# Three column tiles of the second ConvGLU as plain products, with part of the Winograd operands made later

## Chip, cores and metric

The kernel runs on one core of a Trainium2 chip. The metric is the device time of one execution in microseconds (us), median of several. The core has a matrix engine (PE, with its weight loads PEld), VectorE (DVE), ScalarE (ACT), GpSimd (POOL) and SyncE (SP), which here only issues DMAs. Each engine works off its own queue in order; a semaphore wait at the head of a queue holds everything behind it.

## What is computed

Two layers over 512 latent tokens and 256 context tokens of width 1024: layer 0 is windowed attention and a ConvGLU, layer 1 a bidirectional gated recurrence (HGRN) and a ConvGLU. The change is in the ConvGLU of layer 1, on the latent tokens alone:

```
hx2 = rms_norm(x, norm2_g) * (1 + sc2) + sh2          # x: 512 x 1024
gate, val = split(hx2 @ w_up)                         # w_up: 1024 x 5632
u = silu(dwconv3(gate, conv_w, conv_b)) * val         # 512 x 2816
x = x + g2 * (u @ w_down)                             # w_down: 2816 x 1024
```

## The kernel before, in words

Everything lies transposed: features on partitions, tokens along the free dimension. Each fp32 operand is split in two parts, high (`wh`, or index 0 of `hs`) and low (`wl`, index 1), and each product is three matmuls: high by high, high by low, low by high. The high part is a copy on ScalarE, the low part a subtraction on DVE.

The up product has 22 column tiles (`ft`), each with 128 gate columns and 128 value columns. Each is one step of a Strassen-Winograd scheme: the 1024 input features are halved (k below 4, k from 4 on), the tokens are halved (258 columns each, the last of which hold the shift column and padding), and gate and value are the halves of the output. So `gate_pair` (L917) makes 7 products of 4 k-tiles and 3 terms, 84 matmuls of 258 columns, where plain products need 96. The sums on the weights are made by `load_pair` (L121): 7 operands with a high and a low part each (L140, L141) and 4 sums (L136), in a temporary `s1` and in the raw weight buffer `wr` itself. The sums on the activations are made once by `halves` (L361) and `combos` (L386): four quarters of the scaled input (b11, b12 for the first features, b21, b22 for the second; the second index is the token half), and of these seven operands `hs[0..6]`: 0, 1 and 4 are the quarters b11, b21 and b22; 2, 3, 5 and 6 are combinations.

The row factor R (the inverse norm of each token) is only multiplied in after the product, so products can start before the norm is known. `row_factor` (L529) sums the squares on PE (`nss`), takes the power on GpSimd, and spreads the result over the partitions (`dg`, then PE's `nR`, then a copy).

Before this stage, `hgrn_out` (L1297) computes the HGRN output in 4 pairs of row tiles (dp and dp + 4): 8 k-tiles each in PSUM (`ho`), then the residual add into `xl` (L914), then `halves` and the first part of `combos` for the pair, then the squares for the norm. The rest of `combos` (operands 5 and 6) comes after the loop. The `y` buffers of `halves` lie in the pool `ot`, which is closed after the stage; its memory goes on to pools of the ConvGLU.

`ffn` (L964) works in rounds of column tiles, for layer 1 by `ROUNDS[1]` (4, 4, 4, 4, 4, 2). In each round the up tiles of the next round (`up`) alternate with four pairs of down products (`dn`) of the tiles at hand. After a tile's products `up` does the gate's convolution, SiLU and product on ScalarE and DVE and splits the result into `g`. Each up tile loads 1 MB of weights on SyncE's queue into one of two raw buffers (`wr`); the down weights go to `wd` on the same queue. Prepared weight operands rotate through the pools `ws0`, `wsC`, `wsD`, `wsE`. PSUM has 8 banks in two pools of four; `bank` takes them in turn.

The order of the instructions on each queue is not written by hand: a scheduler with its own timing model takes the ready instruction that stands first in the program; weight preparation is moved 180 places forward (`W_AHEAD`). What it fixes is then the order in which the engines run.

Of the kernel before, what the change touches and what calls it, by code (L numbers as in the profile page):

```python
# [9 lines left out]
F32R = mybir.dt.float32r  # L10
BF16 = mybir.dt.bfloat16
AF = mybir.ActivationFunctionType
# [15 lines left out]
NFF = DFF // P  # L28
EPS = 1e-6
NEG = -1e30  # L30
ROUNDS = ((3, 3, 4, 4, 3, 5), (4, 4, 4, 4, 4, 2))
W_AHEAD = 180
PER_UNIT = 3.2

# [34 lines left out]
def f(t):  # L69
    return t.bitcast(F32)  # L70


class Kernel:
# [307 lines left out]
    def put(self, op, kk, src):  # L381

        self.nc.scalar.activation(op[:, 0, kk], src, AF.Copy)  # L383
        self.nc.vector.tensor_tensor(op[:, 1, kk], src, f(op[:, 0, kk]), op=ALU.subtract)

    def combos(self, ys, kk, hs):  # L386


        nc = self.nc
        (b11, b12), (b21, b22) = ys  # L390

        def put(i, src):
            self.put(hs[i], kk, src)

        def diff(o, x, y):
            nc.vector.tensor_tensor(o, x, y, op=ALU.subtract)
            return o

        put(0, b11)
        put(1, b21)  # L400
        put(4, b22)
        t1 = diff(b12, b12, b11)
        put(2, t1)
        t2 = diff(b22, b22, t1)
        put(3, t2)
        yield
        put(5, diff(b21, b21, t2))
        put(6, diff(b11, t2, b11))

    def late_combos(self, l, w, kk, half, hs, pool):  # L410

# [502 lines left out]
            self.nc.vector.scalar_tensor_tensor(x[:, d], ps[:, lo:hi], self.modc(l, v, which, d), x[:, d], op0=ALU.mult, op1=ALU.add)  # L914


    def gate_pair(self, ft, ops, hs, G, gg, R, rows, half, tmp, bank):  # L917


        nc = self.nc  # L920
        Z, Y, V = (bank(x)[:, 0:half] for x in ("pZ", "pY", "pV"))

        def prod(i, ps, first=False):
            self.product(ps, ops[i], lambda k: (hs[i][:, 0, k], hs[i][:, 1, k]), 4, first)

        g = (G[:, 1:1 + half], G[:, 1 + half:1 + 2 * half], gg[:, 0:half], gg[:, half:])
        t0, t2 = (tmp.tile([P, half], F32, tag="t", name="t", bufs=2) for _ in range(2))
        add = lambda o, x, y: nc.vector.tensor_tensor(o, x, y, op=ALU.add)  # L928
        times = lambda eng, o, x, y: eng.tensor_tensor(o, x, y, op=ALU.mult)  # L929

        prod(0, Z, True)
        nc.scalar.activation(t0, Z, AF.Copy)  # L932
        prod(1, Y, True)
        add(g[0], t0, Y)
        prod(3, Z)
        nc.scalar.activation(g[2], Z, AF.Copy)
        next(rows, None)
        if ft == 0:
            prod(2, Z)
            nc.scalar.activation(t2, Z, AF.Copy)  # L940
            prod(4, Z)
            prod(6, V, True)
            nc.scalar.activation(g[3], V, AF.Copy)
            prod(5, V)
        else:
            prod(6, V, True)
            nc.scalar.activation(g[3], V, AF.Copy)
            prod(2, Z)
            nc.scalar.activation(t2, Z, AF.Copy)
            prod(5, V)  # L950
            prod(4, Z)
        add(g[3], g[3], t2)
        add(g[2], g[2], V)
        for _ in rows:
            pass

        times(nc.vector, g[0], g[0], R[:, 0:half])
        times(nc.vector, g[1], Z, R[:, half:])
        times(nc.gpsimd, gg, gg, R)

    def ffn(self, l, hs, R, rows, lat_only, tmp, acp, bk, gp, done, side=None):
# [14 lines left out]
        def up(ft):  # L976

            ws_ = [self.wcols(wup, ft * P, P), self.wcols(wup, DFF + ft * P, P)]
            ops = self.load_pair(ws_, tmp)
            if side:  # L980
                next(side, None)

            G = tmp.tile([P, 2 * half + 2], F32, tag="G", name="G", bufs=gb)
            gg = tmp.tile([P, 2 * half], F32, tag="ny", name="gg", bufs=2)
            self.gate_pair(ft, ops, hs, G, gg, R, rows, half, tmp, bank)
            nc.scalar.activation(ap(G[:, 0:1], 0, (TW + 1, nv)), G[:, 1 + SH:1 + SH + nv], AF.Copy)
            cb = tmp.tile([P, 2], F32, tag="cb", name="cb")
            nc.scalar.activation(cb[:, :nv], G[:, 1 + SH:1 + SH + nv], AF.Identity, scale=ws[:, ft:ft + 1], bias=cw[:, 66 + ft:67 + ft])
            u = tmp.tile([P, n], F32, tag="nt", name="u", bufs=gb)
            nc.scalar.activation(u, G[:, 1:1 + n], AF.Copy, scale=cw[:, 22 + ft:23 + ft])  # L990
            nc.vector.scalar_tensor_tensor(u, G[:, 0:n], cw[:, ft:ft + 1], u, op0=ALU.mult, op1=ALU.add)
            nc.vector.scalar_tensor_tensor(u, G[:, 2:2 + n], cw[:, 44 + ft:45 + ft], u, op0=ALU.mult, op1=ALU.add)
            for v, c, m in segs:
                nc.scalar.activation(u[:, c:c + m], u[:, c:c + m], AF.Silu, bias=cb[:, v:v + 1])
                nc.vector.scalar_tensor_tensor(gg[:, c:c + m], gg[:, c:c + m], gg[:, SH + v:SH + v + 1], u[:, c:c + m],
                                               op0=ALU.subtract, op1=ALU.mult)
            g2 = gp.tile([P, 2, n], F32R, tag="g", name="g")
            nc.scalar.activation(g2[:, 0], gg[:, :n], AF.Copy)  # L998
            nc.vector.tensor_tensor(g2[:, 1], gg[:, :n], f(g2[:, 0]), op=ALU.subtract)
            return g2  # L1000

        f0, late = 0, None
        gt = [up(ft) for ft in range(ROUNDS[l][0])]
        for r, nf in enumerate(ROUNDS[l]):


# [289 lines left out]

    def hgrn_out(self, part, hs, acc, tmp, pj):  # L1297
        nc = self.nc
        some = []
        wout = self.a["hgrn_w_out"][0]  # L1300
        oh = part[0]
        act = lambda k: (oh[:, 0, k], oh[:, 1, k])
        for dp in range(KT // 2):
            if dp < 2:
                w, ps, ks = part[1][dp], part[2][dp], (KT - 1,)
            else:
                w = self.load_w([self.wcols(wout, d * P, P) for d in (dp, dp + 4)])
                ps = pj.tile([P, 1024], F32, tag="pj", name="ho")
                ks = range(KT)
            for j in range(2):  # L1310
                d = dp + 4 * j
                pd = ps[:, 512 * j:512 * j + 512]
                for _ in self.mm_steps(w[j], ks, act, [(pd, 0)], first=dp >= 2):
                    pass
                self.add_gated(1, 2, d, pd, True)
            some.append(self.combos(self.halves(1, 1, dp, 258, True, tmp, ("y0", "y1"), 4), dp, hs))
            next(some[-1])
            for d in (dp, dp + 4):
                self.square_acc(d, acc, True, tmp, "sg", first=(d == 0))
        for rest in some:  # L1320
            for _ in rest:
                pass


    def dump(self, name, t):
# [3 lines left out]
    def run(self, stop=99):  # L1329
# [75 lines left out]
        pj = self.pool(e2, "pj", 2, PSUM)  # L1405
        part = self.hgrn(hn2[0], R, accs[0], hb, pj, lv, sc)
        hc = self.pool(rs, "hC", 1, right=True)
        hs1 = hc.tile([P, 7, 2, 4, 258], F32R, tag="hs", name="hs3")
        hs = [hs1[:, i] for i in range(7)]
        ot = self.pool(es, "ot", 1)  # L1410
        acc = Rp.tile([P, LAT], F32, tag="acc", name="acc2")
        self.hgrn_out(part, hs, acc, ot, pj)
# [94 lines left out]
```

## Time and profile before

| what | us |
|---|---|
| median of 3 runs | 1810.76 |
| lowest and highest run | 1810.32, 1812.5 |
| the profiled execution | 1809.72 |
| its span, first to last instruction | 1807.9 |

In the profile, a row of the timeline gives the start in us from the span's start, the duration, the engine, the line of the kernel, the operation, output and input tile names, and how many instructions it merges; a bracket at its end is the idle time before it and what released it. PE's durations overlap, since matmuls are pipelined: their cost is the distance from start to start. In the stretches by window each engine has its busy time and, in brackets, its number of instructions. PEclk is the clock that was granted to PE as a share of 2.4 GHz.

### The profile page before, as it was taken

To read this page: it belongs to the slowest core of one execution; us is meant where nothing else is said; L and a number is where in the kernel's file an instruction comes from. 1 tells how busy PE (TensorE), PEld (TensorE's weight loads), DVE (VectorE), ACT (ScalarE), POOL (GpSimd) and SP (SyncE) were. 2 spreads that over 40 slices of the span, in tenths; PEclk is the share of its full clock that TensorE was granted. 3 is DMA by queue.
4 is the path that set the end of the run, shared out by engine and by line. 5 is a ranking of instruction groups with operands and counts; after the bars stand their busy time and mean duration, and the time that the engine had idled before them with its cause. 6 is when DMAs were issued, how large, how long until landed. Compare 5 with 4: busy or idle time off the path is not lost.

```text
span 1807.9 us, 32327 instructions
## 1 busy us (share of the span) xinstructions
PE 1760.6 (97%) x13062; PEld 1543.7 (85%) x13062; DVE 1324.9 (73%) x2420; ACT 840.5 (46%) x1754; POOL 248.7 (14%) x233
## 2 busy tenths in 40 slices
PE   6999999999999999999999999999998899999998
PEld 4968785788889989999998888888986689999997
DVE  6576767467768675868877766777776799999985
ACT  4354556555534443534455333333332555555553
POOL 1233333200100010100011110111110011111110
PEclk9999999998999999999999999999999999999999
DMA  9250005232343343312213212111126133433222
GB/s 309 79 200 35 24 1 187 59 105 71 120 126 106 108 131 104 100 47 82 62 52 103 69 48 59 45 51 50 46 71 210 47 106 105 117 106 105 86 68 81
DMA packets 204611, 166.44 MB, mean 92 GB/s; under 512 B 5341, under 2 KB 198446, under 8 KB 199342
## 3 DMA queue, kind: packets, MB, share of 16 engines
q1 hardware_dynamic: 196800, 160.47, 28.9%
q10 hardware_dynamic: 7662, 3.92, 0.8%
q8 instruction: 102, 1.67, 0.4%
q14 instruction: 47, 0.39, 0.1%
HBM read 162.27 MB, written 2.10 MB: 91 GB/s over the span
## 4 chain that ended last, share of the span: by engine, by line
PE 87%; DMA 5%; DVE 5%; ACT 2%; issue 1%; SPq 0%; ACTq 0%; DVEq 0%
PE dn L170 16%; PE pZ L188 15%; PE pf L170 8%; PE pV L188 7%; PE pjq L611 4%; PE pv L170 4%; PE ao L170 4%; PE pY L188 3%; PE pgate L170 3%; PE pq L170 3%; PE pv L844 2%; PE ho L170 2%; PE pt L836 2%; PE kv L611 2%; DMA wr<-in_ffn_w_up 2%; PE ada L309 2%
## 5 line engine op out<-in xcount | busy, mean ns | idle before, releaser
L188 PE MATMUL pZ<-hs,wh 128*128 128x386 f32 (+1 forms) x1408 | 314.1, 314 | 1.1 <-ACT t L932 0.9
L140 ACT ACTIVATE wh<-wr 128x512 fp32r<-128x512 f32 x264 | 162.3, 628 | 229.3 <-PE pZ L188 73.7
L170 PE MATMUL dn<-g,wh 128*128 128x512 f32 (+1 forms) x1056 | 266.9, 358 | 0.4 <-ACT g L998 0.3
L188 PEld LDWEIGHTS pZ<-hs,wh 128*128 128x128 f32 x1408 | 240.7, 191 | 11.5 <-issue 3.4
L117 ACT ACTIVATE wh<-wr 128x512 fp32r<-128x512 f32 (+2 forms) x192 | 113.3, 601 | 292.0 <-PE pf L170 84.0
L141 DVE TENSOR_TENSOR wl<-wr,wh 128x512 fp32r<-128x512 f32 x264 | 189.5, 728 | 47.2 <-ACT wh L140 46.3
L188 PE MATMUL pZ<-hs,wl 128*128 128x386 f32 (+1 forms) x704 | 218.2, 313 | 0.8 <-DVE wl L141 0.8
L170 PEld LDWEIGHTS dn<-g,wh 128*128 128x128 f32 x1056 | 173.4, 188 | 27.6 <-ACT g L998 0.9
L929 POOL TENSOR_TENSOR gg<-gg,R 128x772 f32<-128x772 f32 (+1 forms) x44 | 87.4, 1986 | 722.8 <-DVE gg L928 657.8
L118 DVE TENSOR_TENSOR wl<-wr,wh 128x512 fp32r<-128x512 f32 (+2 forms) x192 | 129.8, 684 | 71.0 <-ACT wh L117 53.5
L188 PE MATMUL pV<-hs,wh 128*128 128x386 f32 (+1 forms) x704 | 161.0, 314 | 1.8 <-ACT hs L383 1.8
L170 PE MATMUL dn<-g,wl 128*128 128x512 f32 (+1 forms) x528 | 160.0, 356 | 0.3 <-DVE wl L118 0.3
L188 PEld LDWEIGHTS pZ<-hs,wl 128*128 128x128 f32 x704 | 133.4, 190 | 3.8 <-DVE wl L141 1.9
L188 PEld LDWEIGHTS pV<-hs,wh 128*128 128x128 f32 x704 | 121.2, 191 | 5.8 <-ACT hs L383 2.1
L170 PE MATMUL pf<-hn,wh 128*128 128x512 f32 (+1 forms) x512 | 117.5, 344 | 0.5 <-ACT v L1114 0.5
L188 PE MATMUL pV<-hs,wl 128*128 128x386 f32 (+1 forms) x352 | 110.2, 314 | 1.3 <-DVE wl L141 1.2
L170 PEld LDWEIGHTS dn<-g,wl 128*128 128x128 f32 x528 | 88.0, 188 | 14.5 <-DVE wl L118 0.5
L1033 DVE SCALAR_TENSOR_TENSOR xl<-dn,mod,xl 128x512 f32<-128x512 f32 x96 | 71.1, 746 | 38.4 <-PE dn L170 38.1
L170 PEld LDWEIGHTS pf<-hn,wh 128*128 128x128 f32 x512 | 79.4, 189 | 12.4 <-ACT v L1114 0.6
L188 PE MATMUL pY<-hs,wh 128*128 128x386 f32 (+1 forms) x352 | 80.8, 315 | 3.9 <-ACT hs L383 3.4
L611 PE MATMUL pjq<-wh,hn 128*128 128x256 f32 x384 | 76.3, 290 | 0.3 <-DVE mod L324 0.3
L188 PEld LDWEIGHTS pV<-hs,wl 128*128 128x128 f32 x352 | 67.1, 191 | 4.5 <-DVE wl L141 1.8
(301 smaller groups left out, 3850.4 us busy)
## 6 DMA issues: line engine op xcount, KB each, us to landing
wr<-in_ffn_w_up SPq DMA_DIRECT2D x88, 512.0 KB, 5.2
wada<-in_ada_w SPq DMA_DIRECT2D x40, 1024.0 KB, 4.8
wr<-in_hgrn_w_in SPq DMA_DIRECT2D x40, 512.0 KB, 4.0
wd<-in_ffn_w_down SPq DMA_DIRECT2D x20, 512.0 KB, 4.0
ar<-in_ada_w SPq DMA_DIRECT2D x32, 256.0 KB, 7.0
wr<-in_attn_w_in SPq DMA_DIRECT2D x6, 1024.0 KB, 8.3
wr<-in_ffn_w_down SPq DMA_DIRECT2D x12, 384.0 KB, 3.0
wr<-in_attn_w_out SPq DMA_DIRECT2D x8, 512.0 KB, 4.0
```

Source lines behind the costliest of these rows:

```text
L117: nc.scalar.activation(wh, src, AF.Copy)
L118: nc.vector.tensor_tensor(wl, src, f(wh), op=ALU.subtract)
L140: nc.scalar.activation(ops[i][0], src, AF.Copy)
L141: nc.vector.tensor_tensor(ops[i][1], src, f(ops[i][0]), op=ALU.subtract)
L170: nc.tensor.matmul(o, lhsT=wt, rhs=at[:, t0:t0 + o.shape[1]], start=(first and n == 0 and i == 0), stop=(last and n == len(ks) - 1 and i = ...
L188: self.nc.tensor.matmul(ps, lhsT=wt, rhs=at, start=(first and k == 0 and i == 0), stop=(k == nk - 1 and i == 2), skip_group_check=not first)
L309: nc.tensor.matmul(ps[32 * j:32 * j + 32, 0:512], lhsT=self.cs[:, k, :], rhs=raw[:, j * 512:(j + 1) * 512], start=(k == 0), stop=(k == KT ...
L611: nc.tensor.matmul(out, lhsT=x, rhs=y[:, wk], start=(start and k == 0 and j == 0), stop=(stop and k == KT - 1 and j == 2))
L836: nc.tensor.transpose(pt[:, j * P:(j + 1) * P], pr[j][:, b * P:(b + 1) * P], self.ident)
L844: nc.tensor.matmul(pv[a * HD:(a + 1) * HD, 0:256], lhsT=V[:, tl, g, :], rhs=pT[:, a * 256:(a + 1) * 256], start=(b == 0), stop=(b == len(t ...
L929: times = lambda eng, o, x, y: eng.tensor_tensor(o, x, y, op=ALU.mult)
L1033: nc.vector.scalar_tensor_tensor(x[:, d], o, self.modc(l, v, 5, d), x[:, d], op0=ALU.mult, op1=ALU.add)
```

## The change

In layer 1 alone:

- The first three column tiles (`PLAIN = 3`) take plain products (`gate_plain`) with ordinary weight operands (`load_w`: 4 of 512 columns, high and low) instead of a Winograd step. For gate and value each, two PSUM tiles (one per token half) are accumulated side by side over 8 k-tiles, in the order 0, 4, 1, 5, 2, 6, 3, 7. R is multiplied in at the end of the value product, for gate and value, by four DVE operations that read PSUM.
- They read the quarters straight: `hs` has eight operands now, and b12 stands in `hs[7]`. The quarters are made in `hgrn_out` by `quadrants`, from `xl` into high and low part without the intermediate `y`; shift columns and padding of the second token half once by `quadrant_shifts`.
- `combos` makes only operands 2, 3, 5 and 6 there (`quadrants=False`), with `halves` into buffers of the `g` pool, issued in the program ahead of column tile 0 (pairs 0 and 1) and ahead of tile 1 (pairs 2 and 3).
- `ROUNDS[1]` is (3, 4, 4, 4, 4, 3).
- The scratch memory that the compiler reserves for DMAs is cut to 1024 bytes a partition.

```diff
-ROUNDS = ((3, 3, 4, 4, 3, 5), (4, 4, 4, 4, 4, 2))
+ROUNDS = ((3, 3, 4, 4, 3, 5), (3, 4, 4, 4, 4, 3))
+PLAIN = 3
...
-        put(0, b11)
-        put(1, b21)
-        put(4, b22)
+        if quadrants:
+            put(0, b11)
+            put(1, b21)
+            put(4, b22)
...
+    def quadrants(self, l, w, d, half, hs):
+        nc = self.nc
+        sc = self.gs[l][:, 0, 8 * w + d:8 * w + d + 1]
+        for op, t0, n in ((hs[1 if d >= 4 else 0], 0, half), (hs[4 if d >= 4 else 7], half, LAT - half)):
+            x, h = self.xl[:, d, t0:t0 + n], op[:, 0, d % 4, 0:n]
+            nc.scalar.activation(h, x, AF.Copy, scale=sc)
+            nc.vector.scalar_tensor_tensor(op[:, 1, d % 4, 0:n], x, sc, f(h), op0=ALU.mult, op1=ALU.subtract)
+
+    def quadrant_shifts(self, l, w, half, hs):
+        nc = self.nc
+        c = SH - half
+        for op, d in ((hs[7], 0), (hs[4], 4)):
+            sh = ap(self.mod[l][:, 0, 24 * w + d:24 * w + d + 1], 0, (1, 4), (48, 2))
+            y = op[:, 0, :, c:c + 2]
+            nc.scalar.activation(y, sh, AF.Copy)
+            nc.vector.tensor_tensor(op[:, 1, :, c:c + 2], sh, f(y), op=ALU.subtract)
+            nc.gpsimd.memset(f(op[:, :, :, c + 2:]), 0.0)
...
+    def gate_plain(self, ft, ops, hs, G, gg, R, rows, half, tmp, bank):
+        nc = self.nc
+        quad = ((hs[0], hs[1]), (hs[7], hs[4]))
+        for j, dst in enumerate((G[:, 1:1 + 2 * half], gg)):
+            ps = [bank("pd")[:, 0:half] for _ in range(2)]
+            for k in (0, 4, 1, 5, 2, 6, 3, 7):
+                wh, wl = (t[:, k % 4 * P:k % 4 * P + P] for t in ops[j][k // 4])
+                for i, (wt, part) in enumerate(((wh, 0), (wh, 1), (wl, 0))):
+                    for o, q in zip(ps, quad):
+                        nc.tensor.matmul(o, lhsT=wt, rhs=q[k // 4][:, part, k % 4], start=(k == 0 and i == 0), stop=(k == 7 and i == 2))
+            next(rows, None)
+            if j:
+                for _ in rows:
+                    pass
+            if j:
+                for d, outs in zip((G[:, 1:1 + 2 * half], gg), (keep, ps)):
+                    for t, o in enumerate(outs):
+                        nc.vector.tensor_tensor(d[:, t * half:(t + 1) * half], o, R[:, t * half:(t + 1) * half], op=ALU.mult)
+            keep = ps
...
-            ops = self.load_pair(ws_, tmp)
+            plain = lat_only and ft < PLAIN
+            ops = self.load_w(ws_) if plain else self.load_pair(ws_, tmp)
...
-            self.gate_pair(ft, ops, hs, G, gg, R, rows, half, tmp, bank)
+            (self.gate_plain if plain else self.gate_pair)(ft, ops, hs, G, gg, R, rows, half, tmp, bank)
...
-        gt = [up(ft) for ft in range(ROUNDS[l][0])]
+        gt = []
+        for ft in range(ROUNDS[l][0]):
+            if lat_only:
+                for kk in ((0, 1), (2, 3), ())[ft]:
+                    for _ in self.combos(self.halves(1, 1, kk, half, True, gp, ("g", "g"), 9), kk, hs, False):
+                        pass
+            gt.append(up(ft))
...
-        some = []
+        self.quadrant_shifts(1, 1, 258, hs)
...
-            some.append(self.combos(self.halves(1, 1, dp, 258, True, tmp, ("y0", "y1"), 4), dp, hs))
-            next(some[-1])
             for d in (dp, dp + 4):
+                self.quadrants(1, 1, d, 258, hs)
                 self.square_acc(d, acc, True, tmp, "sg", first=(d == 0))
-        for rest in some:
-            for _ in rest:
-                pass
...
-        hs1 = hc.tile([P, 7, 2, 4, 258], F32R, tag="hs", name="hs3")
-        hs = [hs1[:, i] for i in range(7)]
+        hs1 = hc.tile([P, 8, 2, 4, 258], F32R, tag="hs", name="hs3")
+        hs = [hs1[:, i] for i in range(8)]
```

## Rows read from the trace of the kernel before

**Rows 1.** The page, part 1: busy time and instructions of each engine.
```profile
PE 1760.6 (97%) x13062; PEld 1543.7 (85%) x13062; DVE 1324.9 (73%) x2420; ACT 840.5 (46%) x1754; POOL 248.7 (14%) x233
```
**Rows 2.** Busy time by window; after POOL come PEclk, DMA share, GB/s.
```profile
1200.00:1220.00 20.00, 20.00 (x248) 17.73 (x248) 13.14 (x20) 7.75 (x17) 1.51 (x1) 1.00 0.19 54
1440.00:1460.00 20.00, 14.88 (x86) 13.75 (x85) 18.43 (x38) 10.97 (x23) 3.01 (x1) 0.74 0.18 58
1460.00:1480.00 20.00, 18.60 (x149) 17.82 (x148) 17.36 (x30) 11.79 (x24) 3.58 (x2) 1.00 0.46 120
1480.00:1500.00 20.00, 19.43 (x158) 18.96 (x157) 19.71 (x35) 14.87 (x33) 1.75 (x1) 1.00 0.32 87
1449.00:1455.00 6.00, 6.00 (x29) 6.00 (x30) 6.00 (x15) 2.29 (x5) 3.01 (x1) 0.51 0.00 0
```
**Rows 3.** PE's waits, 1400 to 1500: total us, times, longest.
```profile
PE pY L188 <- ACT hs L383: 3.4, 1, 3.4
PE nss L536 <- DVE acc L527: 1.7, 1, 1.7
PE ho L170 <- DVE xl L914: 1.6, 2, 1.2
PE pV L188 <- DVE wl L141: 1.2, 1, 1.2
PE pZ L188 <- DVE wl L141: 0.6, 1, 0.6
```
**Rows 4.** Timeline of PE after the HGRN output.
```profile
1447.50 1.87 PE L536 MATMUL nss<-cst,acc 128*128 128x2 f32 x8 [1.75 <-DVE acc L527]
...
1450.45 0.63 PE L188 MATMUL pV<-hs,wh 128*128 128x258 f32 x2
...
1451.09 0.63 PE L188 MATMUL pV<-hs,wh 128*128 128x258 f32 x2
...
1457.61 0.40 PE L188 MATMUL pY<-hs,wh 128*128 128x258 f32 x2
...
1457.97 0.40 PE L188 MATMUL pY<-hs,wh 128*128 128x258 f32 x2
```
**Rows 5.** Timeline of PE in the HGRN projections.
```profile
1203.15 0.64 PE L170 MATMUL pgate<-hn,wh 128*128 128x256 f32 x4
...
1205.06 0.41 PE L170 MATMUL pgate<-hn,wl 128*128 128x256 f32 x2
1205.31 0.95 PE L1236 MATMUL oss<-cst,osq 128*128 128x2 f32 x8
```
**Rows 6.** Timeline of DVE after the HGRN output.
```profile
1440.76 0.69 DVE L136 TENSOR_TENSOR s<-wr 128x512 f32<-128x512 f32 x1 [0.63 <-PE ho L170]
...
1447.96 0.76 DVE L384 TENSOR_TENSOR hs<-y,hs 128x258 fp32r<-128x258 f32 x2
...
1449.84 1.28 DVE L141 TENSOR_TENSOR wl<-wr,wh 128x512 fp32r<-128x512 f32 x2
```
**Rows 7.** DVE's groups by form, 1440 to 1800: busy us, mean ns; idle before.
```profile
L991 DVE SCALAR_TENSOR_TENSOR u<-G,par,u 128x512 f32<-128x512 f32 x22 | 16.3, 743 | 0.6 <-ACT u L990 0.6
...
L384 DVE TENSOR_TENSOR hs<-y,hs 128x258 fp32r<-128x258 f32 x7 | 2.8, 418 | 0.0
```
**Rows 8.** Waits of SyncE's queue, 1380 to 1530: total us, times, longest.
```profile
SPq L95 <- DVE hs L384: 54.3, 2, 33.3
```
**Rows 9.** Timeline of SyncE's queue, 1380 to 1510.
```profile
1455.44 0.92 SPq L95 DMA_DIRECT2D wd<-in_ffn_w_down  x2
1457.85 45.22 SPq L95 DMA_DIRECT2D wr<-in_ffn_w_up  x10
```
**Rows 10.** Timelines of DVE and POOL where they meet.
```profile
1462.96 1.55 DVE L141 TENSOR_TENSOR wl<-wr,wh 128x512 fp32r<-128x512 f32 x1 [0.44 <-ACT wh L140]
...
1462.67 1.29 POOL L929 TENSOR_TENSOR gg<-gg,R 128x516 f32<-128x516 f32 x1 [8.04 <-DVE gg L928]
```
**Rows 11.** Timeline of DVE, the last up tile.
```profile
1779.52 0.43 DVE L929 TENSOR_TENSOR G<-pZ,R 128x258 f32<-128x258 f32 x1 [0.36 <-PE pZ L188]
...
1785.79 0.68 DVE L999 TENSOR_TENSOR g<-gg,g 128x512 fp32r<-128x512 f32 x1
```

More of the change, by code (lines that the diff above doesn't have):

```diff
@@ L384, in put, with combos @@
         self.nc.vector.tensor_tensor(op[:, 1, kk], src, f(op[:, 0, kk]), op=ALU.subtract)
-    def combos(self, ys, kk, hs):
+    def combos(self, ys, kk, hs, quadrants=True):
         nc = self.nc
@@ L1493 @@
     from concourse.bass_utils import run_bass_kernel_spmd
-    nc = bacc.Bacc("TRN2", target_bir_lowering=False, num_devices=1)
+    nc = bacc.Bacc("TRN2", target_bir_lowering=False, num_devices=1, dynamic_dma_scratch_size=1024)
     arrays, args = {}, {}
```

## The prediction

> **What bounds the kernel now.** I read the page's first part: the tensor engine (PE) is busy for 97% of the span, so time can come only from what it computes and from its few holes [rows 1]. The windows show where the holes are. Away from the change's place PE fills its 20 us (1200 to 1220); around the handover from the HGRN output to the second ConvGLU, 1440 to 1480 us, it is busy 14.88 and 18.60 of 20 us, and in the first of these its granted clock is 0.74 of full [rows 2]. The other columns say why: VectorE (DVE) is busy 17 to 20 of 20 us there, ScalarE at most 15.
>
> The waits give names and sizes [rows 3]. PE stands 3.4 us at the second product (pY) for ScalarE's write of `hs`, the operand that `combos` makes, and 1.7 us at the sum of squares (`nss`) for DVE. That is 5.1 us. After 1455 it stands another 2.5 us, 1.8 of it for low parts of weights. PE's own rows give the third loss [rows 4]: between 1449 and 1455 the granted clock is 0.51, the lower of its two levels (1.2 instead of 2.4 GHz), to which it fell in the 3.4 us wait. Three 258-column matmuls then take 0.64 us (1450.45 to 1451.09) instead of 0.36 (1457.61 to 1457.97), so 0.094 us more each; of the 29 in that window [rows 2] 27 lie whole in it, 2.5 us. The eight `nss` matmuls took 1.87 us, and an equal eight (`oss`) at full clock 0.95 [rows 5], so 0.9 more. Clock loss 3.4 us.
>
> **Losses at the handover: 5.1 + 2.5 + 3.4 = 11.0 us.**
>
> Why DVE is late can be counted. Back to back, a second 128x512 operation adds 0.60 us (1.28 - 0.68) and a 128x258 one 0.34 us (0.76 - 0.42) [rows 6]. From the end of the HGRN output (1440.8) until the fourth column tile (ft 3) can start, DVE must do: weight operands of four pairs, 11 each (7 low parts, 4 sums), less 2 done earlier: 42 x 0.60 = 25.2; the 7 writes and 3 differences of `combos` still open [rows 7]: 3.4; five gate operations for each of three tiles: 15 x 0.34 = 5.1; convolution and split of two tiles, 4 operations, 2.6 us each: 5.2; residual, acc, R and small ones: 2.2. Sum 41.1 us. PE has 3 x 84 matmuls of 0.1195 us, 30.1, and 1.9 for `nss` and `nR`: 32.0. DVE is 9 us longer, near the 11.0 lost. A DMA chain sits in it too: SyncE's queue stood up to 33.3 us until DVE had made its last `hs` from `y` [rows 8] (the tile for down weights, `wd`, lies where `y` lay), and the next up weights, queued behind, were issued only at 1457.85 [rows 9].
>
> **The change part by part.**
>
> *Plain products, ft 0 to 2.* 2 outputs x 8 k x 3 split terms x 2 token halves = 96 matmuls instead of 84, all of 258 columns: 3 x 12 x 0.1195 = **+4.3 us** of PE, on the path. That the two halves alternate between two PSUM banks under one weight tile costs nothing: `pgate` does just that with 256 and 258 columns, and its 16 matmuls from 1203.15 to 1205.06 take 0.119 us each [rows 5].
>
> *Weights of these tiles.* Four 512-column operands instead of seven, no sums: DVE saves 7 x 0.60 = 4.2 us a tile. They need no buffer in `tmp`, which in before could not be written until the last `ho` matmul (the first sum waits for it until 1440.76 [rows 6]). All four operands of ft 0 use buffers that the third pair of HGRN outputs frees, so they should be ready by 1431.
>
> *Operands.* In `hgrn_out`, each pair of row tiles loses two `y`, their shift columns, seven writes and four differences, and gains four ScalarE scalings and four DVE subtractions of 254 to 258 columns. Such a subtraction, with scale, is not in the trace; it lies between 0.42 (128x258 plain) and 0.75 us (128x512 with scale [rows 7]); I take 0.45, by the size. So DVE has 1.8 us per pair of tiles instead of 11 x 0.34 = 3.7. That stage is PE's: nothing gained but the wait for `xl` (1.2 us, 1415.4 to 1416.6 [rows 3]), of which I count 0. The shift helper adds two ScalarE, two DVE and two GpSimd instructions of a few columns, once, early in the stage.
>
> *Combinations moved.* 16 differences and 16 writes, 32 x 0.34 = 10.9 us of DVE, now lie after the handover, with some 10.6 us on ScalarE, which has over 5 us free in each 20 [rows 2]. Their cover is the 34.4 us in which PE does the plain tiles; nobody needs `hs` 2, 3, 5 and 6 before ft 3. Their `y` buffers are `g` slots (9); eight `y` and `dg` fill these, but the first four `y` are free before the first `g` is written. GpSimd gets eight fills of two columns in its queue, ahead of its power for R; it has hardly other work there.
>
> *Gate.* Four DVE products instead of five operations, no ScalarE copies, and three of GpSimd's products (the first 1.29 us) fall away; a DVE operation that met one took 1.55 us instead of 0.68 [rows 10]. Worth up to 3 x 0.9 us of DVE, off the path; I count 0.
>
> *SyncE's queue.* `y` leaves the place under `wd`, so the 33 us wait goes. A raw weight buffer of ft 0 is read out at about 1431, so ft 2's weights are issued then instead of at 1457.85.
>
> DVE's sum after: weights 4 + 4 + 11 = 19 x 0.60 = 11.4; combinations 10.9; gates 12 x 0.34 = 4.1; convolutions 5.2; last quarters 4 x 0.4 = 1.6; the rest 2.2. **35.4 us against PE's 34.4 + 1.9 = 36.3.** DVE no longer sets the start of ft 3; PE does.
>
> *What is late next.* After the last `ho` matmul the last two quarters need a residual (0.75), a scaling (about 0.4) and a subtraction (0.45), with handover gaps about 2.4 us. PE has, ready by then, k = 0, 1, 2, 4, 5, 6 for both outputs: 72 matmuls, 8.6 us, less what it takes into earlier holes. R comes by `nss`, GpSimd's power, `dg`, `nR` and a copy; only the gate operations of ft 0 wait for it, and while four banks hold their inputs ft 1 begins in others. So the 3.4 and 1.7 us waits should go and the clock stay at 1.00. In place of all 11.0 us I leave 1.5, between 0.3 (none but a little in the down products) and 4.2 (the 2.4 us chain uncovered and the `nss` wait again).
>
> *Rounds.* 3,4,4,4,4,3 instead of 4,4,4,4,4,2: the same 528 down matmuls, 48 residuals and weight bytes. The third tile of the last round is now followed by one pair of downs of round five, 24 matmuls of 512 columns, by size 24 x 0.237 = 5.7 us, while from its gate to `g` took 7 us (1779.5 to 1786.5 [rows 11]). The missing 1.3 us are covered by first and second k of the last round, 1.4 us for each output and eight banks for them. I count 0, at worst 1.3. The DMA scratch setting only makes room for the eighth operand: the kernel issues its DMAs on SyncE's and ScalarE's queues; 0.
>
> **Sum.** -11.0 + 4.3 + 1.5 = -5.2 us. Span 1807.9 to 1802.7. The profiled execution took 1809.72, 1.8 us above its span, so 1804.5; the median of the three runs lies 1.0 us above the profiled one, so 1805.5.
>
> **Rivals.**
>
> *A, the handover stands again.* PE's queue is in order: if a matmul of the last quarters or `nss` is placed ahead of those that are ready, PE waits as at pY. Then 3.4 us of wait and 3.4 us of low clock return; saved remain 1.7 + 2.5 = 4.2 against 4.3: about 1810.7. For it: `nss` stood so in before with other matmuls behind it. Against: 8.6 us of ready work, and `before` could not split the weights so early.
>
> *B, slower: DVE becomes the bound of the plain tiles.* The margin is 0.9 us in 36. In 1440 to 1480 DVE was busy 35.8 of 40 us [rows 2]; with such holes 35.4 becomes 39.6, ft 3 starts 3.3 us late, and with delayed `y` buffers or weights it can be twice that, 6.6; in a stall like that at pY the clock falls as it did there, 3.4 more. Net -11.0 + 4.3 + 6.6 + 3.4 = +3.3, and with the late `g` of the last round (1.3) +4.6: 1815.4. It decides from a 6.5 us stall at ft 3. Against: combinations are issued ahead of most weights, and the first two products of ft 3 need only two operands.
>
> *C, alternating banks disturb the clock.* PE would run the 288 plain matmuls at 0.214 instead of 0.1195 us: +27, 1832 us. The `pgate` stretch with its alternation had a clock of 1.00 [rows 2]. The Trainium skill, TensorE: Matmul & The Clock Gate, section on a second failure mode by PSUM-queue depth-cycling, tells of a kernel whose clock oscillated as it cycled through banks; this trace disagrees.
>
> *D, the change does not do what it says:* the scheduler puts the combinations ahead of the plain tiles' work on DVE and ScalarE, so PE still waits for them. The time is that of A, and its chance is in A's.
>
> **How the numbers follow.** Forecast 63% (1803 to 1807, residual up to 3.1), A with the larger residuals 26%, B 9%, C 1%, 1% left. 0.2% is 3.6 us, about what a measurement of this kernel tells from no change. Faster (under 1807.1) 0.63, same 0.27, slower 0.10. Low end: residual 0.3 and the `xl` wait gone, 1803.1, rounded down; high end takes in A: 1810.8.
>
> **What would show it.** Right: PE waits between 1440 and 1480 under 2 us in all, clock 1.00 there, about 36 more matmuls in the count, up weights of ft 2 issued before 1445, DVE's waits for ft 3 short. Wrong: a wait of PE on `hs` at the first tile or on `wl` at ft 3, clock under 1, or new PE waits on `g` after 1780.

## The result, and the profile after

| | before | after |
|---|---|---|
| median of 4 runs each, us | 1811.06 | 1798.78 |
| lowest and highest run | 1810.32, 1812.5 | 1796.57, 1803.25 |
| the profiled execution | 1809.72 | 1796.57 |
| its span | 1807.9 | 1794.6 |

After against before is 0.9931, interval 0.9919 to 0.9944: 12.3 us faster, between 10.1 and 14.7. The forecast was 5.3 us, 1810.76 to 1805.5, and its low end was 1803.1, rounded down. The direction was right, the gain is more than twice what was forecast, and the time lies below the low end. The profiled execution of after is its fastest run, so the 13.1 us between the two profiles are not the gain; below, stretches inside the traces are compared instead.

The page's first part, after (against [rows 1]):
```profile
PE 1755.2 (98%) x13098; PEld 1542.7 (86%) x13098; DVE 1313.5 (73%) x2402; ACT 835.6 (47%) x1739; POOL 244.0 (14%) x232
```
PE does 36 matmuls more, as counted, and has 13.3 us less of span to do them in. Busy time by window around the handover, after (columns as in [rows 2]):
```profile
1420.00:1440.00 20.00, 20.00 (x107) 17.02 (x105) 14.18 (x28) 10.21 (x20) 0.00 (x0) 1.00 0.58 150
1440.00:1460.00 20.00, 20.00 (x164) 19.52 (x163) 17.68 (x40) 12.52 (x31) 1.54 (x9) 1.00 0.19 54
1460.00:1480.00 20.00, 20.00 (x158) 19.51 (x157) 18.76 (x42) 15.53 (x38) 0.00 (x0) 1.00 0.26 73
1480.00:1500.00 20.00, 20.00 (x146) 18.96 (x145) 19.62 (x36) 12.02 (x24) 1.31 (x1) 1.00 0.26 74
```
PE is busy in all of each 20 us where it was busy 14.88 and 18.60, and the granted clock is 1.00 where it was 0.74. DVE is as full as before, so it was not made idle; it is no longer waited for. The waits of PE from 1405 to the end, after, are one line (before has eight over the same stretch, five of them in [rows 3]):
```profile
PE ho L171 <- DVE xl L937: 1.6, 2, 1.3
```
That is the wait for `xl` inside the HGRN output, which the prediction left where it was. Timeline of PE at the handover and at the start of column tile 3, after (against [rows 4]):
```profile
1434.94 0.40 PE L171 MATMUL ho<-oh,wl 128*128 128x512 f32 x1
1435.17 0.65 PE L951 MATMUL pd<-hs,wh 128*128 128x258 f32 x4
1435.66 0.41 PE L951 MATMUL pd<-hs,wl 128*128 128x258 f32 x2
1435.90 0.64 PE L951 MATMUL pd<-hs,wh 128*128 128x258 f32 x4
...
1440.96 0.28 PE L951 MATMUL pd<-hs,wh 128*128 128x258 f32 x1
1441.08 0.95 PE L559 MATMUL nss<-cst,acc 128*128 128x2 f32 x8
1441.88 0.61 PE L951 MATMUL pd<-hs,wh 128*128 128x258 f32 x3
...
1448.34 1.02 PE L568 MATMUL nR<-dg,cst 128*128 128x512 f32 x2
...
1471.29 0.41 PE L951 MATMUL pd<-hs,wl 128*128 128x258 f32 x2
1471.54 0.41 PE L189 MATMUL pZ<-hs,wh 128*128 128x258 f32 x2
```
The first plain matmul starts 0.23 us after the last `ho` matmul, six of them take 0.73 us (1435.17 to 1435.90, 0.12 each, in two banks in turn), `nss` now comes 0.12 us behind the matmul ahead of it and takes 0.95 us instead of 1.87, and the Winograd tile 3 follows the plain ones without a gap. SyncE's queue, after (against [rows 9]); each tile has two transfers, so the first two of these four are the weights of column tile 2, the others those of tile 3:
```profile
1431.15 4.67 SPq L96 DMA_DIRECT2D wr<-in_ffn_w_up  x4
```

### The same stretch in both traces

Everything that was edited for PE's order lies between two rows that both kernels have: the first matmul of the third pair of HGRN outputs, and the last down matmul. Timeline of PE, before (rows not shown so far), then after:
```profile
1416.64 0.72 PE L170 MATMUL ho<-oh,wh 128*128 128x512 f32 x2 [1.20 <-DVE xl L914]
...
1441.51 0.29 PE L188 MATMUL pY<-hs,wl 128*128 128x258 f32 x1
1445.17 0.58 PE L188 MATMUL pY<-hs,wh 128*128 128x258 f32 x1 [3.37 <-ACT hs L383]
...
1800.95 0.40 PE L170 MATMUL dn<-g,wl 128*128 128x512 f32 x1
```
```profile
1412.67 0.73 PE L171 MATMUL ho<-oh,wh 128*128 128x512 f32 x2 [1.26 <-DVE xl L937]
...
1787.69 0.39 PE L171 MATMUL dn<-g,wl 128*128 128x512 f32 x1
```
Start to start this is 384.31 us before and 375.02 us after: **9.3 us shorter**. From the last down matmul to the end of the span both take 6.9 us. The remaining 4.0 us of the difference between these two spans lie ahead of the stretch, where no instruction of PE was edited, though their order changed (below); the section on the experiments comes back to that.

### The profile page after: what moved, and what is told of

Read it like the earlier page. It is cut to its first block, busy times and chain, and to the rows that moved or that the text cites. A ratio compares the mean times of both kernels' runs of the same rounds, so it can differ in the third digit from the quotient of the medians.

```text
span 1794.6 us, 32375 instructions
## 1 busy us (share of the span) xinstructions
PE 1755.2 (98%) x13098; PEld 1542.7 (86%) x13098; DVE 1313.5 (73%) x2402; ACT 835.6 (47%) x1739; POOL 244.0 (14%) x232
## 4 chain that ended last, share of the span: by engine, by line
PE 93%; DMA 3%; DVE 2%; ACT 1%; issue 0%; SPq 0%; ACTq 0%; DVEq 0%
PE dn L171 17%; PE pZ L189 16%; PE pV L189 8%; PE pf L171 8%; PE pjq L634 4%; PE pY L189 4%; PE pv L171 4%; PE ao L171 4%; PE pgate L171 3%; PE pq L171 3%; PE pv L867 3%; PE pt L859 2%; PE ho L171 2%; PE ada L310 2%; PE kv L634 2%; PE pd L951 2%
## 5 line engine op out<-in xcount | busy, mean ns | idle before, releaser
L189 PE MATMUL pZ<-hs,wh 128*128 128x386 f32 (+1 forms) x1312 | 295.2, 315 | 1.0 <-ACT t L977 0.7
L141 ACT ACTIVATE wh<-wr 128x512 fp32r<-128x512 f32 x246 | 152.5, 629 | 224.5 <-PE pZ L189 78.7
L189 PEld LDWEIGHTS pZ<-hs,wh 128*128 128x128 f32 x1312 | 225.1, 190 | 11.4 <-issue 3.4
L142 DVE TENSOR_TENSOR wl<-wr,wh 128x512 fp32r<-128x512 f32 x246 | 178.9, 736 | 47.9 <-ACT wh L141 47.1
L189 PE MATMUL pZ<-hs,wl 128*128 128x386 f32 (+1 forms) x656 | 204.3, 314 | 0.3 <-DVE wl L142 0.2
L119 DVE TENSOR_TENSOR wl<-wr,wh 128x512 fp32r<-128x512 f32 (+2 forms) x204 | 138.1, 685 | 72.2 <-ACT wh L118 54.7
L189 PE MATMUL pV<-hs,wh 128*128 128x386 f32 (+1 forms) x656 | 150.7, 315 | 1.8 <-ACT hs L384 1.8
L189 PEld LDWEIGHTS pZ<-hs,wl 128*128 128x128 f32 x656 | 123.7, 189 | 2.6 <-DVE wl L142 0.9
L189 PEld LDWEIGHTS pV<-hs,wh 128*128 128x128 f32 x656 | 113.0, 190 | 5.3 <-ACT hs L384 2.1
L823 POOL TENSOR_SCALAR P<-P,r 128x512 f32<-128x512 f32 (+1 forms) x64 | 53.6, 842 | 95.4 <-DVE r L822 79.3
```

What stands on the lines that cost most here:

```text
L119: nc.vector.tensor_tensor(wl, src, f(wh), op=ALU.subtract)
L141: nc.scalar.activation(ops[i][0], src, AF.Copy)
L142: nc.vector.tensor_tensor(ops[i][1], src, f(ops[i][0]), op=ALU.subtract)
L189: self.nc.tensor.matmul(ps, lhsT=wt, rhs=at, start=(first and k == 0 and i == 0), stop=(k == nk - 1 and i == 2), skip_group_check=not first)
L823: nc.gpsimd.tensor_scalar(p[:, :n], p[:, :n], r[:, j:j + 1], 1.0, op0=ALU.mult, op1=ALU.mult)
```

## The experiments

The first experiments asked which of the edits carries the gain, since it was larger than the sum. The theory was that the handover's losses had been counted too low; the rivals were the smaller DMA scratch memory, which moves every tile in SBUF and with it the order of the instructions from 76 us on, and a result that does not repeat. "Stretch" is always that of the last section.

**The scratch memory alone, in before.**
```diff
-num_devices=1)
+num_devices=1, dynamic_dma_scratch_size=1024)
```


> The kernel before with nothing changed but the DMA scratch, cut to 1024 bytes a partition. Theory (layout): in the changed kernel's profile the third pair of HGRN outputs begins 4.0 us earlier (1412.7 instead of 1416.6), though nothing in front of it was edited; the freed 15 KB shift the pools, which changes what waits for whose memory and so the order that the scheduler fixes from some 76 us on. Then this kernel alone is 2 to 4 us faster than before, 1807 to 1809, and its handover at 1440 is as bad as in before (waits of 3.4 and 1.7 us, clock 0.5). Rival (chance): the 4 us are the luck of one execution, the changed kernel's fastest; then this kernel is within 1 us of before.

1811.59 us beside 1812.69 of before on that chip, ratio 0.9996 (0.9985 to 1.0007), stretch 384.24. In the stretch the scratch memory carries nothing, and the 2 to 4 us of the theory do not show in the time. Ahead of the stretch the traces do show something. With the smaller scratch PE's matmuls run in another order between some 80 and 450 us. Two rows of PE that have the same matmuls between them in both orders, before, then this run:
```profile
169.73 0.66 PE L836 MATMUL pt<-cst,Pc 128*128 128x128 f32 x4
...
398.51 0.82 PE L902 MATMUL xT<-cst,xs 128*128 128x128 f32 x6
```
```profile
169.51 0.66 PE L836 MATMUL pt<-cst,Pc 128*128 128x128 f32 x4
...
397.54 0.82 PE L902 MATMUL xT<-cst,xs 128*128 128x128 f32 x6
```
Start to start this is 228.78 and 228.03 us. Over all fourteen traces the five with the old order (four of before, and after with the larger scratch of the next run) take 228.78 to 229.25, the nine with 1024 bytes 227.71 to 228.03: the means differ by 1.2 us and the two groups do not overlap. The timed runs, 1.1 us apart by their medians, are too coarse to show it.

**The scratch memory larger, in after.**
```diff
-dynamic_dma_scratch_size=1024
+dynamic_dma_scratch_size=12288
```


> The changed kernel with a DMA scratch of 12288 bytes, the least cut by which it fits, so that the instruction order up to the HGRN layer is nearly that of before. Theory (layout): what the first 1400 us gained goes back, and the gain of the stage itself stays, 9 us in the profiles: about 1802. Rival (chance): as the changed kernel, 1799, within 1 us.

1800.76 us, ratio 0.9939 (0.9925 to 0.9952), stretch 375.02, that of after to the hundredth. The rival by layout falls from both sides as far as the stretch goes. Ahead of it this run has before's order and before's time again: 229.25 us between the two rows above, where after takes 227.77. So the layout carries about 1.2 of the 12.3 us, and none of the 9.3.

**After once more.**

> The changed kernel again, beside its variants on the same chip: 1797 to 1801. Its runs spread from 1796.6 to 1803.3; if one mode of that spread is an early loss (a lower clock or a DMA wait in front of 1400 us), a profile of a slower execution shows it there, and the stretch from the third pair of HGRN outputs to the end stays at 382 us.

1799.66 us, 0.9933 (0.992 to 0.9945), stretch 375.06. The result repeats. Its profiled execution is 3.1 us longer than that of after, and all of it lies ahead of the stretch, which starts at 1415.75 instead of 1412.67. One difference there is the clock, after, then this run:
```profile
1395.00:1412.00 17.00, 15.19 (x68) 11.31 (x65) 8.45 (x20) 6.50 (x14) 1.17 (x3) 1.00 0.31 90
```
```profile
1395.00:1412.00 17.00, 15.89 (x72) 12.68 (x71) 6.08 (x15) 3.49 (x9) 1.17 (x3) 0.90 0.27 67
```
Such a spell of low clock stands there in nine of the fourteen traces, of before and of after's kind alike.

**Two plain tiles instead of three.**
```diff
-PLAIN = 3
+PLAIN = 2
```


> Two plain column tiles instead of three (the third is a Winograd pair again). PE loses 12 matmuls, 1.43 us; DVE gains 7 operations of 0.60 us, 4.2 us. Theory (DVE is no longer the bound): DVE had 35.4 us of work against 36.3 of PE with three plain tiles by the prediction's count, and PE stood nowhere for it; with two plain tiles the fourth tile's start asks 39.9 of DVE against 34.9 of PE, so PE waits up to 5 us for weights or combinations at the third tile: 0 to 4 us slower than three. Rival (cover is ample): PE still waits nowhere and the time falls by 1.4 us.

1806.7 us, 0.997 (0.9958 to 0.9982), stretch 382.93: 7.9 us longer than after though it has 12 matmuls (1.4 us) less. PE's waits in it, 1410 to 1805:
```profile
PE pZ L189 <- DVE hs L385: 2.0, 1, 2.0
PE ho L171 <- DVE xl L937: 1.6, 2, 1.3
PE pV L189 <- DVE hs L385: 1.1, 2, 0.7
PE pZ L189 <- ACT t L977: 1.1, 1, 1.1
PE pV L189 <- ACT wh L141: 0.5, 1, 0.5
PE pY L189 <- DVE wl L142: 0.2, 1, 0.2
```
and its window behind the first of these:
```profile
1476.00:1484.00 8.00, 7.26 (x37) 7.05 (x37) 7.96 (x17) 4.20 (x10) 0.00 (x0) 0.57 0.43 121
```
PE waits for the combinations that now lie behind the handover (`hs`, line 385) and the clock falls to 0.57, near its lower level, right after those waits. The waits without `xl` sum to 4.9 us, and the count of DVE's work made its excess here 5.0. This is rival B's mechanism, one tile away from the change: with two plain tiles DVE, and in part ScalarE, hold up the products of the first Winograd tiles, with three nothing does. Start to start the stops are 6.6 us, the low clock costs 2.5 more.

**Before, a second profile.**

> The kernel before, a second profile of it. In the two profiles so far of this instruction order (before, and the same with the small scratch) the stretch from the third pair of HGRN outputs to the last down matmul is 384.3 and 384.2 us, against 375.0 in three profiles of the changed one: 9.3 us, while the timed runs differ by 12 to 13. If the handover varies from execution to execution (longer low clock, later weights), this profile shows a longer stretch, 385 to 388; if it is 384.3 again, the rest of the difference lies in front of the stretch.

1809.15 us, stretch 385.93: 1.6 longer than in the first profile. Its clock is 0.74 in 1440 to 1460, as in [rows 2], and it falls a second time:
```profile
1470.00:1480.00 10.00, 8.79 (x55) 8.18 (x56) 9.75 (x17) 7.18 (x15) 2.28 (x1) 0.83 0.34 98
```
So what before loses to the clock differs from execution to execution.

**Three plain tiles, but all combinations made in the HGRN output stage.**
```diff
-                for kk in ((0, 1), (2, 3), ())[ft]:
-                    for _ in self.combos(self.halves(1, 1, kk, half, True, gp, ("g", "g"), 9), kk, hs, False):
-                        pass
+                pass
...
                 self.square_acc(d, acc, True, tmp, "sg", first=(d == 0))
+            for _ in self.combos(self.halves(1, 1, dp, 258, True, tmp, ("y0", "y1"), 4), dp, hs, False):
+                pass
```


> Plain products and eight operands as in the changed kernel, but the 16 differences and 16 writes of the combinations stay in the HGRN output stage, each pair's behind its squares, with their buffers in the pool that ends up under the down weights. Theory (moving the combinations carries the gain): they fill DVE and ScalarE ahead of the last quarters and weights and hold SyncE's queue at the down weights, so PE waits at the handover, 3 to 6 us, and the clock falls: 1804 to 1808. Rival (the plain products carry it, and the place of the combinations doesn't matter): nobody reads them before the fourth tile, so 1799 to 1801, as the changed kernel.

1799.46 us, 0.9938 (0.9926 to 0.9951), stretch 374.89, no wait of PE but `xl`. Its timeline of SyncE's queue shows `wd`, which lies where `y` lay, issued late again, and the up weights behind it:
```profile
1420.56 19.23 SPq L96 DMA_DIRECT2D wr<-in_ffn_w_up  x6
1451.37 0.90 SPq L96 DMA_DIRECT2D wd<-in_ffn_w_down  x2
1453.17 20.46 SPq L96 DMA_DIRECT2D wr<-in_ffn_w_up  x6
```
and it costs nothing. Counted from the start of the stretch (1418.20 here, 1412.67 in after), the weights of tile 3 are issued after 35.0 instead of 21.5 us (1453.17 against 1434.15); those of tile 2, the last two of the first six, after 20.6 instead of 18.5:
```profile
1438.80 0.99 SPq L96 DMA_DIRECT2D wr<-in_ffn_w_up  x2
```
This was against my theory, in which the moved combinations were a part of the gain: the plain products on the quarters bring all of it. No run has the new quarters without plain tiles, so these two are shown together only.

**Four plain tiles.**
```diff
-PLAIN = 3
+PLAIN = 4
```


> Four plain column tiles instead of three. By the prediction's price of a plain tile, 12 matmuls of 0.1195 us, it is 1.4 us slower than three (about 1801.2), since PE stands nowhere in the stretch already. Rival (DVE still sets the pace somewhere that PE's rows don't show): the 4.2 us of DVE that a plain tile saves win something back, and it is no slower than three.

1803.11 us, 0.9956 (0.9944 to 0.9968), stretch 376.26: 1.24 us longer than after, against 12 x 0.1195 = 1.43 for twelve more matmuls. The fourth plain tile is all cost, so nothing was left to win at the start of tile 3.

**Two plain tiles, the combinations of two pairs made in front of the handover.**
```diff
-PLAIN = 3
+PLAIN = 2
...
-                for kk in ((0, 1), (2, 3), ())[ft]:
+                for kk in ((2, 3), (), ())[ft]:
...
                 self.square_acc(d, acc, True, tmp, "sg", first=(d == 0))
+        for kk in (0, 1):
+            for _ in self.combos(self.halves(1, 1, kk, 258, True, tmp, ("y0", "y1"), 2), kk, hs, False):
+                pass
```


> Two plain tiles, with the combinations of the first two pairs of row tiles made in the HGRN output stage, behind its loop, where DVE has 5.8 of 20 us free in the changed kernel's trace; those of the other two stay after the handover. Theory (with two plain tiles the 4.9 us of waits at the third tile, 1476, were DVE's excess of 39.9 against 34.9): 5.4 us of DVE taken out of the way close it, the waits go, the clock stays, and it runs at 1798.3 to 1799, 1.4 us below three plain tiles at best. Rival (the handover itself is tight): the work in front delays the last quarters or the squares, and PE waits at 1440 instead; 1802 to 1807.

1798.92 us, 0.9936 (0.9921 to 0.9951), stretch 373.49. All stops of the two-tile run above are gone, and the twelve matmuls that it saves show in full (375.02 - 373.49 = 1.5). Its windows:
```profile
1440.00:1460.00 20.00, 20.00 (x164) 19.52 (x163) 19.33 (x45) 13.25 (x32) 1.31 (x5) 1.00 0.20 55
1460.00:1480.00 20.00, 20.00 (x160) 19.60 (x160) 19.77 (x37) 13.97 (x28) 1.49 (x1) 1.00 0.43 124
```
Only the making of two pairs' combinations, on DVE and ScalarE, was moved between the two runs with two plain tiles, and 9.4 us went: that work behind the handover decides, and DVE's part of it is what the prediction counted. By its trace this kernel is 1.5 us better than after; the timed runs can't tell the two apart.

**One plain tile, all combinations in front** (the edit of the run with all combinations in front, and one line more).

```diff
-PLAIN = 3
+PLAIN = 1
```


> One plain tile, the combinations all in the HGRN output stage (as in the run that left them in front). With them in front DVE has, from the handover to the start of ft 2, two pairs' weights (22 x 0.60 = 13.2), a plain gate and a pair's (3.1), one convolution (2.6) and 3.8 of rest, 22.7 us, against PE's 11.5 + 10.0 + 1.9 = 23.4. Theory (balance of DVE against PE): no waits, the stretch loses 2 x 1.2 us against three plain tiles: 372.5 us, 1797 to 1798. Rival (one tile does not bridge the handover: its 11.5 us are over before the second tile's sums and products are made): waits of 2 us or more at the second or third tile, with a spell of low clock: 1801 to 1806.

1800.34 us, 0.9941 (0.9926 to 0.9956), stretch 375.02 where 372.5 was expected. PE waits again:
```profile
...
PE pZ L189 <- DVE wl L142: 1.3, 2, 0.8
PE pZ L189 <- ACT wh L141: 0.4, 1, 0.4
```
Start to start the stops are 2.9 us, as much as the 24 matmuls that it saves (2.87). One plain tile does not quite bridge the time in which DVE and ScalarE split the seven operands of each of the next ones (the three waits end at 1452.34, 1472.08 and 1484.82).

**The old rounds, in after.**
```diff
-ROUNDS = ((3, 3, 4, 4, 3, 5), (3, 4, 4, 4, 4, 3))
+ROUNDS = ((3, 3, 4, 4, 3, 5), (4, 4, 4, 4, 4, 2))
...
-                for kk in ((0, 1), (2, 3), ())[ft]:
+                for kk in ((0, 1), (2, 3), (), ())[ft]:
```


> The changed kernel with the rounds of before (4, 4, 4, 4, 4, 2). By the prediction the rounds are worth 0 (at worst 1.3 us the other way): 1799 to 1801, the stretch from the third pair of HGRN outputs to the last down matmul at 375.0 us. Rival (the shorter first round carries a part of the gain, since down products fill PE one tile earlier): the stretch is 1 us or more longer, with waits of PE between 1460 and 1500.

1798.62 us, 0.9936 (0.9924 to 0.9948), stretch 374.80. The rounds are worth nothing either way.

**Before, two more profiles.**

> The kernel before, a third profile. The stretch from the third pair of HGRN outputs to the last down matmul was 384.3, 384.2 (small scratch) and 385.9 us (with a second spell of low clock at 1473). If the spells vary in this way, this one is 384 to 387, and their mean, not the one profile that the prediction read, is the loss that the change takes away.

> The kernel before, a fourth profile, as the one ahead of it: 384 to 387 us for the stretch; the start of the third pair of HGRN outputs anywhere from 1412 to 1418, since profiles of both kernels spread so far.

1816.05 and 1811.16 us, stretches 384.39 and 385.31. The stretch varies by 1.7 us over five executions that have before's order in it (mean 384.8, the run with the smaller scratch memory among them). The two longest, 385.93 and 385.31, are the two with a second spell of low clock: 0.91 in 1460 to 1480, where the other three have 1.00. The clock is not all of it: the first of these two profiles has a shorter first spell than the others (0.83 in 1440 to 1460 against 0.74) and is yet no shorter; against that stand two waits that the first profile lacks:
```profile
PE pV L188 <- DVE hs L384: 0.4, 1, 0.4
...
PE nR L545 <- DVE dg L541: 0.3, 1, 0.3
```
What lies ahead of the stretch varies more. Its first matmul starts at 1414.45 to 1422.93 us in these five, at 1412.67 to 1418.20 in the nine runs of after and its variants; the latest has the clock at 0.83 there:
```profile
1400.00:1420.00 20.00, 17.62 (x70) 13.72 (x68) 6.62 (x15) 4.80 (x10) 1.31 (x9) 0.83 0.28 69
```

All variants side by side; each gain is against before, the timed one by the medians on the same chip, the other by 384.8 less its stretch:

| kernel | plain tiles, combinations | stretch, us | gain in it | timed gain |
|---|---|---|---|---|
| after | 3, behind | 375.02 | 9.8 | 12.3 |
| after again | 3, behind | 375.06 | 9.7 | 13.0 |
| larger scratch | 3, behind | 375.02 | 9.8 | 11.9 |
| old rounds | 3, behind | 374.80 | 10.0 | 12.3 |
| combinations in front | 3, in front | 374.89 | 9.9 | 11.1 |
| four plain tiles | 4, behind | 376.26 | 8.5 | 7.4 |
| two plain tiles | 2, behind | 382.93 | 1.9 | 6.0 |
| two, half in front | 2, both | 373.49 | 11.3 | 11.6 |
| one plain tile | 1, in front | 375.02 | 9.8 | 10.6 |

## Why the prediction was off

**The failed step: "Losses at the handover: 5.1 + 2.5 + 3.4 = 11.0 us", and behind it the 1.5 left over.** The mechanism was right, two sizes were not. Read from start to start of neighbouring matmuls instead of from idle time, before loses 14.0 us in the stretch: the 9.3 by which after is shorter, the 4.3 of its added matmuls and the 0.4 that it still loses. By places:

| term | forecast | start to start |
|---|---|---|
| stops at pY and `nss` | 5.1 | 3.5 + 2.2 = 5.7 |
| later stops | 2.5 | 3.6 |
| clock | 3.4 | 3.5 |
| the remainder, each too small to be a wait | none | 1.1 |
| all | 11.0 | 14.0 |

The rows show why. The wait at pY is 3.37 us, but the two starts lie 3.66 us apart (1441.51 to 1445.17) where 0.12 is due: 3.54. In front of `nss` the wait is 1.75 us and the starts lie 2.33 apart (1445.17 to 1447.50): 2.21. A wait is counted from the modelled end of the last matmul, and in a filled pipeline the next would have started before that end: 3.37 + 0.29 = 3.66, and 1.75 + 0.58 = 2.33. (The matmul ahead of `nss`, at 1445.17, took 0.58 us where 0.29 is usual, at the low clock, so 0.29 of the 2.21 is the clock's.) The clock's 3.5 is the 7.45 us from the first `nss` to the first matmul at full clock (1447.50 to 1454.95), less the 0.80 that `nss` takes to the next start in after and 26 x 0.12. The later stops are six such places: five small waits, 3.2 us start to start, and the entry of `nR`, 0.4, which no wait row has. The 1.1 was not measured by itself; it makes the sum come out. Its places can be named: next to the later stops other distances are longer too, as here the one behind the wait of 0.57 (0.22 us where 0.12 is usual):
```profile
1491.08 0.39 PE L188 MATMUL pZ<-hs,wl 128*128 128x258 f32 x1 [0.57 <-DVE wl L141]
1491.30 0.40 PE L188 MATMUL pZ<-hs,wh 128*128 128x258 f32 x2
```
Twelve such distances, 0.10 to 0.18 us over the usual one, lie between 1471 and 1574 in before, 1.4 us in all; after has none there.

Of the 1.5 us that the prediction left for what would be late next, 0.4 remain: the entry of `nR` (1448.34), in both kernels. So the stretch is -14.0 + 4.3 + 0.4 = -9.3, against -11.0 + 4.3 + 1.5 = -5.2 in the forecast: 3.0 us of losses missed and 1.1 left over too many. Both errors had the same sign, and the low end of the range took the 11.0, and the 1.2 of the `xl` wait, as all there was to win; no bound stood behind that number. A third term was too small ahead of the stretch: the scratch memory, put at 0, brought about 1.2 us there.

**What is still missing.** Timed, the change brings 12.3 us (10.1 to 14.7), the stretch 9.3 to 9.8. Over the nine kernels of the table the timed gain exceeds that of the stretch by 1.7 us on average, from -1.1 to +4.1. No instruction was edited for PE ahead of the stretch, and its start there scatters by 5.5 us over nine executions and by 8.5 over five; the means, 1415.5 and 1417.7 us, differ by 2.3, more than half of it by the one late execution. Of this the smaller scratch memory carries about 1.2 us, by the two rows that were compared above (1.0 of the 4.0 us between the first two profiles, which differ in the clock as well: 0.90 in 1395 to 1412 in before, 1.00 in after); its timed gain in before (1.1 us, with an interval from -1.3 to 2.7) agrees and would not show it alone. The stretch and this come to 9.8 + 1.2 = 11.0 us, inside the interval of the timed gain. Whether the last 1.3 us are real, or the runs merely fell so, stays open.

**The steps that held.**
- *Plain products cost 4.3 us and no more.* 36 more matmuls, 0.12 us each in two banks in turn; the fourth plain tile measured 1.24 us for a price of 1.43.
- *DVE's count.* 36.3 us were forecast from the last `ho` matmul to tile 3; PE started it 36.4 us after the first plain matmul (1435.17 to 1471.54). DVE's last combination is written at that time too:
```profile
1472.13 0.42 DVE L385 TENSOR_TENSOR hs<-y,hs 128x258 fp32r<-128x258 f32 x1
```
That row starts after tile 3 has begun. DVE and PE are level, so of the margin of 0.9 us nothing is left, but PE has no wait there; with two plain tiles the same count gave 5.0 us of excess, and 4.9 of waits came (3.3 of them for DVE, 1.6 for ScalarE, which the count left out, so that the closeness is in part luck).
- *The new subtraction.* Taken as 0.45 us; 0.48 by DVE's groups by form, after, 1405 to 1790:
```profile
L420 DVE SCALAR_TENSOR_TENSOR hs<-xl,gs,hs 128x258 fp32r<-128x258 f32 x8 | 3.9, 483 | 0.0
```
- *The `xl` wait and the rounds at 0.* The wait stands (1.6 us in all, before and after); the rounds have a run of their own. The scratch memory is 0 in the stretch alone.
- *The weights of tile 2 at 1431.* Issued at 1431.15. The 33 us wait ahead of `wd` [rows 8] is gone, but the queue still waits long behind the combinations, now ahead of later tiles' weights; after, 1420 to 1500:
```profile
SPq L96 <- DVE hs L385: 33.0, 2, 23.7
```
PE does not wait for it. Nor did the early issue carry the gain as far as a run shows it: with the combinations in front the weights of tile 3 come 13.5 us later in the stretch, those of tile 2 2.1 us, and the stretch is as long. Weights of tile 2 as late as before's were not tried with plain tiles.

**The rivals.** A and D would have shown as waits on `hs` and a clock under 1 at the first plain tile; there is neither, because `nss` and the last quarters were placed behind ready matmuls. B did not occur in after, but it is real one tile further: the run with two plain tiles shows its waits, its place and its clock. C did not occur: the 288 plain matmuls ran at 0.12 us with a granted clock of 1.00. The Trainium skill, TensorE: Matmul & The Clock Gate, section on a second failure mode by psum-queue depth-cycling, tells of another kernel whose clock oscillated as it cycled through banks and PE went idle for short times between groups of matmuls; here PE alternates between two banks without idle times and its clock stays at 1.00, as in the `pgate` stretch ([rows 2] and [rows 5]).

**Which part of the change pays.** Going by the stretches: one plain tile with the combinations in front takes 9.8 us away; a second, with half of them in front, 1.5 more (373.49); a third only costs its 1.5, and is needed only where all combinations lie behind the handover. Moving them is no gain here: with three plain tiles both places give the same, with two the later place loses 9.4 us.

## What to carry to other kernels

Price a stop of a busy matrix engine from the starts of the matmuls on both sides, less their usual distance, and not from its row among the waits; and look for losses that have no wait row before a sum of waits is taken as all there is to win. When operands that need much preparation stand at the head of a stage, a few products on simple operands there are a bridge: count, tile by tile, the preparing engine's work against the bridge's length, and make it no longer than that. When a kernel varies by some us where nothing was changed, compare the stretch between two rows that both traces have; and do the same ahead of the edit, since a change of memory layout alone can reorder what was not edited (here 1.2 us that the timed runs did not show).

## What the runs showed of the hardware

- A stop costs PE more than its idle time: 3.54 us for a wait of 3.37, 2.21 for one of 1.75 (0.29 of it the low clock).
- The clock's fall at the same stops is not the same in each execution of one kernel: 0.74 or 0.83 in 1440 to 1460, and 1.00 or 0.91 in 1460 to 1480. The two executions with 0.91 have the longest stretches, 385.31 and 385.93 us; the three with 1.00 take 384.24 to 384.39. In after and in all variants without such stops the stretch repeats to 0.04 us where the program is the same (375.02, 375.06).
- The start of the stretch lies anywhere from 1414.45 to 1422.93 us over four executions of before, one and the same program, with a clock of 0.80 to 1.00 in 1395 to 1412.
